# A one-core encoder layer on Trainium2: turning the gated features on VectorE and by transfers inside SBUF instead of on TensorE, with fewer seven-product pairs

## The chip, the core and the metric

The kernel runs on one core of one Trainium2 chip. A core has TensorE (PE in the profile; its weight loads are listed as PEld), VectorE (DVE), ScalarE (ACT), GpSimd (POOL) and SyncE (SP, which here only issues DMAs), sixteen DMA engines, a software-managed SBUF of 128 partitions, and PSUM, in which matmuls accumulate. The metric is the device time of one execution in microseconds (us). Several runs were taken of the kernel before, and one further execution was profiled; the trace has the start and the end of every instruction of that one.

## What is computed

One layer of an encoder for 256 positions (S) with 2048 features (D), all in float32:

```
u      = rms_norm(h) @ w_in                      # 2048 x 5120
mixed  = concat(rms_norm(attention), rms_norm(recurrence)) @ w_out
h      = h + rms_norm(mixed)
fn     = rms_norm(h)
ff     = (silu(fn @ w_gate) * (fn @ w_up)) @ w_down      # 2048 -> 5632 -> 2048
h      = h + rms_norm(ff)
h      = h + rms_norm(sigmoid(rms_norm(h) @ w_ple_gate) * (p @ w_ple_proj))
```

The change touches the line with `w_gate`, `w_up` and `w_down` (the FFN). Its middle features, silu(gate) * up, come out with positions on the partitions, and `w_down` needs them with features on the partitions: they have to be transposed.

## The kernel before

**Products.** Each float32 operand is split in a rounded part `hi` and the rest `lo`, and a product is three matmuls: hi by hi, hi by lo, lo by hi. A weight tile is 256 rows by 512 columns (128 partitions x 1024 elements, 512 KB). SP loads it into a raw slot (L439), ACT makes `wh` (L464), DVE makes `wl` (L489), and PE uses both (L528 to L530). Raw slots ("wr") and split slots ("w") are few and are lent and given back through the kernel; a load waits for a raw slot, and a cast for a split slot.

**Groups.** The FFN works in groups of two weight chunks of 512 columns (gate and up, or two chunks of w_down). A group takes its 256-row steps, called units or pairs, one after another. A "p" unit is plain: two weight tiles, 24 matmuls of 512 columns. An "s" unit forms the same 2 x 2 blocks of products by seven products in place of eight (`seven`, L546): 21 matmuls, but two further weight tiles, which DVE makes as sums and differences of the first two (`sum_stream`, L509 and L513, four subtractions of 512 elements), and which have to be cast and split as well. On the side of the activations such a unit needs four sums of position blocks (`act_sums`). `KINDS` says which of the eight units of a gate/up group are "s", and `DOWN` gives order and kind of the units of a down group.

**The FFN's order.** Eleven gate/up groups (`Gated`) in three parts: groups 0 to 3, 4 to 7 and 8 to 10. After each part come two down groups (`Down`) for the features just made; after the last part one down group and two plain chunks.

**The end of a gate/up group.** `Seven.early` and `Gated.late` add up what the seven products left in PSUM (L1553 to L1565, L1589), put silu on the gate half (L1616) and multiply with the up half (L1596), all with positions on the partitions. Then `transposed` (L307) has PE turn the result in blocks of 128 x 128 into a PSUM bank, four at a time (L315), twice a group, and `split` (L292) makes hi and lo of each bank (ACT L295, DVE L297). For the "s" units of the down groups, `mid_sums` adds hi and lo again (L1390) and forms the four sums (L1466) and their hi and lo.

**What sets the order.** The program's instruction order on each engine is made by a planner (`Plan`) when the kernel is built. It has a clock for each engine with estimated costs; a step is a generator that yields (engine, cost, slot to take or give), and of all steps that could go the one that starts earliest is taken, with `late` added to its start (a negative value brings it forward). On the chip each engine then works through its instructions strictly in that order and waits by semaphores where the real times differ from the planned ones. This holds for SP too: all loads and stores of the layer go through its one queue in planned order.

Of the kernel before, what the change touches and what calls it, by code (L numbers as in the profile page):

```python
# [43 lines left out]
for _n, _w in (  # L44
# [23 lines left out]
LATE_SUMS = 0.0  # L68
FIRST = "ppppspsp"
KINDS = "ppspspsp"  # L70
HALF = max(2 * KINDS.count("s") * 4 * P, 2 * 1024)
# [156 lines left out]

def dma(kb, take=None):
    return ("dma", kb / 340.0, None, take, None)  # L230
# [3 lines left out]
def layer(ctx: ExitStack, tc: tile.TileContext, a: dict, out: bass.AP):  # L234
# [6 lines left out]
        wr=R_BUFS, w=W_BUFS, ts=0, acc=ACC_BUFS, sm=SM_BUFS, ev=1, mid=2, bt=2, uv=1  # L241
# [36 lines left out]
    ones = const.tile([P, P], F32, name="ones")  # L278
    nc.gpsimd.memset(ones, 1.0)
# [50 lines left out]
    def done(event):  # L330
        event.t = plan.now
# [11 lines left out]
    class Act:  # L343
# [10 lines left out]
        def blocks(self, hi, lo, base, n, first=0):  # L354
            for i in range(n):
                self.at[base + i] = (hi[:, first + i, :], lo[:, first + i, :])
# [18 lines left out]
    class Group:  # L375


        def __init__(self, w, n0, lhs, ks, kinds, post, after=None):
            self.after = after
            self.lhs, self.post, self.banks, self.i0 = lhs, post, {}, len(tiles)  # L380
            self.early = Event()
            self.units = list(zip(ks, kinds))
            self.early = Event()
            for (k, _), kind in self.units:
                i = len(tiles)
                tiles.extend((w[c], k, n0[c]) for c in range(2))
                by_dma.update({"d": (i, i + 1), "e": (i + 1,), "c": (i,)}.get(kind, ()))
                if kind == "s":
# [82 lines left out]
    def add_raw(i):  # L471
        yield added(512)
        nc.gpsimd.dma_start(los[i], raws[i], accum_op=ALU.add)
        landed = Event()
        landed.t = plan.now + LANDED
        yield landed
        done(ev_lo[i, 2])
        used(i)
# [40 lines left out]
    def products(i, kx, lhs, accs, ts, start, stop, at=0.0):  # L519
        for j in range(2):  # L520
            here = ev_lo[i, j + 1] if (i, j + 1) in ev_lo else ev_lo[i, 2]
            plan.main(6 * MM * len(ts) / NT, here, lhs.ev[kx + j], at=at)
            wh, wl = his[i], los[i]
            hi, lo = lhs.at[kx + j]
            for t in ts:
                sl = slice(t * P, (t + 1) * P)
                st, sp = start and j == 0, stop and j == 1
                nc.tensor.matmul(accs[t], hi[:, sl], wh[:, j, :], start=st, stop=False)  # L528
                nc.tensor.matmul(accs[t], hi[:, sl], wl[:, j, :], start=False, stop=False)  # L529
                nc.tensor.matmul(accs[t], lo[:, sl], wh[:, j, :], start=False, stop=sp)  # L530
            at_pe[0] = max(at_pe[0], i)
            if j:
                free_w(i)
            plan.run()
# [11 lines left out]
    def seven(i, kx, g, start, stop):  # L546

        for name, v, j, which in FORMS:
            n = i + v
            if isinstance(which, tuple):  # L550
                kk, t = which
                (hi, lo), ev = g.lhs.at[kx + kk], g.lhs.ev[kx + kk]
                hi, lo = hi[:, t * P : (t + 1) * P], lo[:, t * P : (t + 1) * P]
# [14 lines left out]
    def run_group(g, flip):  # L568
# [5 lines left out]
        strassens = [n for n, (_, kind) in enumerate(g.units) if kind == "s"]  # L574
        for n, ((_, kx), kind) in enumerate(g.units):
            if kind == "s":
                seven(i, kx, g, n == strassens[0], n == strassens[-1])
                i += 4
                if n == strassens[-1]:
                    plan.add(g.post.early(g), plan.clk["pe"] + plan.SEM)  # L580
                    plan.run()
                continue
# [7 lines left out]
        plan.add(g.post.late(g), plan.clk["pe"] + plan.SEM)  # L590
# [139 lines left out]
    def open_p1():  # L730
        t1["hs"], t1["rec_hi"] = big(0, "hs", F32), big(1, "rec_hi")
        p1 = p1_ctx.enter_context(tc.tile_pool(name="p1", bufs=1))
        t1["pool"] = p1
        xp = p1.tile([P, HB, S + 4], F32, name="xp")
# [23 lines left out]
        nc.gpsimd.memset(ssr, 0.0)  # L758
# [3 lines left out]
    ssr = const.tile([P, S], F32, name="ssr")  # L762
    ssa = const.tile([P, S], F32, name="ssa")
# [151 lines left out]
    def group_rstd(ss, name):  # L915
# [3 lines left out]
        nc.tensor.matmul(pb[:, 0, :], ones, ss, start=True, stop=True)  # L919
        rb = const.tile([P, S], F32, name=f"rb_{name}")  # L920
# [15 lines left out]
    def gate_pair(b0, b, e, ev):  # L936
# [9 lines left out]
        yield from add_squares(ssr, sq, False)  # L946
        done(ev)

    def yg_post(hf):
        def post(ch):  # L950
# [13 lines left out]
            rb = yield from group_rstd(ssr, "rec")  # L964
# [132 lines left out]
    def attend(g):  # L1097
        ph, pl, vh, vl, sq, attnT = (t1[n] for n in ("ph", "pl", "vh", "vl", "sqa", "attnT"))
        yield ev_v[g]
        for b in range(0, HB, 2):  # L1100
# [23 lines left out]
            yield from add_squares(ssa, sq, h == 0)  # L1124
# [3 lines left out]
        ra = yield from group_rstd(ssa, "attn")  # L1128
# [39 lines left out]
    def open_p2():  # L1168
# [12 lines left out]
        for n in range(W_MORE):  # L1181
# [3 lines left out]
            plan.free["w"].append(plan.clk["pe"])  # L1185
        plan.add(load_p2(), plan.clk["pe"])
# [191 lines left out]
    def mid_sums(mid, ks):  # L1378
        rs = t2["pool"]
        a_ = rs.tile([P, 2, 2, 4, P], F32R, tag="ple0", name="sums_a")  # L1380
        b_ = rs.tile([P, 2, 4, P], F32R, tag="pT", name="sums_b")
        at_ = [(a_[:, n, 0, :, :], a_[:, n, 1, :, :]) for n in range(2)]
        at_.append((b_[:, 0, :, :], b_[:, 1, :, :]))
        for k, (hi, lo) in zip(ks, at_):
            mid.sums[k] = hi, lo
            yield mid.ev[k]
            yield mid.ev[k + 1]
            yield dve(2 * S, take="uv")
            v = at.tile([P, 2, NT, P], F32, tag="at0_hi", name="v")
            nc.vector.tensor_tensor(  # L1390
                out=v.rearrange("p k t m -> p k (t m)"), in0=f32(mid.pair_of(k, 0)),
                in1=f32(mid.pair_of(k, 1)), op=ALU.add,
            )
            yield from act_sums(mid, k, v)

# [18 lines left out]
    def transpose_h(b, hi, lo, nxt, gname):  # L1414
# [20 lines left out]
        yield from act_sums(nxt, b, v)  # L1435
# [20 lines left out]
    def act_sums(x, b, v):  # L1456

        s = at.tile([P, 4, P], F32, tag="at0_lo", name="s")
        for n, i0, i1, op in (
            (0, v[:, 0, 1, :], v[:, 1, 1, :], ALU.add),  # L1460
            (1, s[:, 0, :], v[:, 0, 0, :], ALU.subtract),
            (2, v[:, 0, 0, :], v[:, 0, 1, :], ALU.subtract),
            (3, v[:, 1, 0, :], s[:, 1, :], ALU.subtract),
        ):
            yield dve(P)
            nc.vector.tensor_tensor(out=s[:, n, :], in0=i0, in1=i1, op=op)  # L1466
# [63 lines left out]
    class Mid(Act):  # L1530
        def __init__(self, name):
            super().__init__()
            self.name, self.halves = name, {}
# [8 lines left out]
        def pair_of(self, k, which):  # L1542
            i, j = divmod(k, 8)
            return self.halves[i][which][:, j : j + 2, :]
# [31 lines left out]
    class Gated(Seven):  # L1576
# [5 lines left out]
        def late(self, g):  # L1582
# [3 lines left out]
            gated = [Event() for _ in range(NT)]  # L1586
            for t, c, n, x in self.parts():
                yield dve(N)
                nc.vector.tensor_tensor(out=x, in0=bk[n], in1=x, op=ALU.add)  # L1589
                g.give(n)  # L1590
                if not c:
                    plan.add(self.silu(t, gated[t]), plan.now)
            for t in range(NT):
                yield gated[t]
# [4 lines left out]
                )  # L1599
            plan.free["uv"].append(plan.now)  # L1600
            for b in range(0, 4, 2):
                tr = yield from transposed(e, b, g.ring["c11"])
                if b == 2:
                    plan.free["mid"].append(plan.now)
                kk = self.kk0 + b
                i, j = divmod(kk, 8)
                hi, lo = self.mid.tiles(i)
# [5 lines left out]
        def silu(self, t, ev):  # L1613
# [34 lines left out]
    hF.ev_sums = {k: Event() for k, kind in zip(ORDER, KINDS) if kind == "s"}  # L1648

    parts = ((0, 4), (4, 8), (8, 11))  # L1650
    for part, (f0, f1) in enumerate(parts):
        mid = Mid(f"mid{part}")
        for f in range(f0, f1):
            Group(("w_ffn_gate", "w_ffn_up"), (f * N, f * N), hF,
                  [(k, k) for k in ORDER], KINDS if f else FIRST, Gated(mid, (f - f0) * 4))
        last_lent[0] = len(tiles)
        last = part == len(parts) - 1
        units = [[(u[0], int(u[1:])) for u in us.split()] for us in DOWN[f1 - f0]]
        summed = []
        for us in units[:1] if last else units:  # L1660
            summed += [k for kind, k in us if kind == "s" and k not in summed]
        mid.ev_sums = {k: Event() for k in summed}
        for n in range(1 if last else 2):
# [3 lines left out]
                  after=(lambda mid=mid, ks=summed: plan.add(  # L1667
                      mid_sums(mid, ks), plan.clk["pe"], LATE_SUMS)) if n == 0 else None)
# [189 lines left out]
```

## Time and profile before

| what | value |
|---|---|
| runs before (three) | 1175.58, 1175.52, 1174.06 us, median 1175.52 us |
| the profiled execution, its own time | 1173.45 us |
| its span, first to last instruction | 1171.7 us |
| mean granted TensorE clock | 0.997 |
| ACT busy | 701.9 us, 60% of the span |
| DMA queue of SP | 237.79 MB, 60.9% of sixteen engines' span |
| FFN groups | about 377 us to 1055 us of the span |

The profile lists instructions by source line and by tile names, written as output<-inputs. "idle before" is the time that an engine stood still just before such instructions, with what ended the wait. Matmuls overlap in the trace (each is shown as 0.39 us long, though a new one starts every 0.23 us), so for PE it is the distance of the starts that counts.

### The profile page before, as it was taken

The numbers are of one execution on the slowest core, as the hardware profiler recorded it, in microseconds if no ns is written. First come the engines' busy times: TensorE is split into PE (matmuls) and PEld (weight loads), VectorE is DVE, ScalarE is ACT, GpSimd is POOL, SyncE is SP. The second block draws the span as 40 slices with busy tenths as digits, with TensorE's granted clock in tenths as the row PEclk, the third lists the DMA queues.
The fourth block names the chain that finished last, engine by engine and source line by source line (L and its number), as shares of the span: only waits on it lengthen the run. The fifth ranks groups of instructions, "written<-read, shape, count | busy, mean of one in ns | idle before, by whom it ended". The sixth has DMA issues, their size and how long they took to land.

```text
span 1171.7 us, 14652 instructions
## 1 busy us (share of the span) xinstructions
PE 1150.5 (98%) x5259; PEld 951.6 (81%) x5259; DVE 961.3 (82%) x1267; ACT 701.9 (60%) x952; POOL 1.6 (0%) x13
## 2 busy tenths in 40 slices
PE   7999999999999999999999999999999999999996
PEld 5788888888888888888888888888888888887885
DVE  5677868778549898898989899889999989888663
ACT  6787777766548655563665556554536446466752
POOL 0000000000000000000000000000000000000000
PEclk9999999999999999999999999999999999999998
DMA  8855555545864865664775475575567456775751
GB/s 307 288 173 180 176 187 197 164 158 168 313 229 141 302 191 180 224 214 146 226 256 192 159 245 182 173 238 160 191 207 242 153 180 229 261 246 190 241 171 72
DMA packets 70344, 238.80 MB, mean 204 GB/s; under 512 B 7552, under 2 KB 13824, under 8 KB 68864
## 3 DMA queue, kind: packets, MB, share of 16 engines
q1 hardware_dynamic: 70128, 237.79, 60.9%
q8 instruction: 41, 0.67, 0.2%
q14 instruction: 31, 0.25, 0.1%
q10 hardware_dynamic: 144, 0.08, 0.0%
HBM read 232.60 MB, written 5.24 MB: 203 GB/s over the span
## 4 chain that ended last, share of the span: by engine, by line
PE 82%; DVE 6%; DMA 6%; ACT 3%; issue 1%; SPq 1%; DVEq 0%; ACTq 0%
PE c L528 12%; PE c L530 12%; PE c L529 12%; PE acc L530 9%; PE acc L528 9%; PE acc L529 9%; PE p L538 3%; PE p L539 3%; PE p L537 3%; DVE wl L489 3%; PE c L537 2%; PE c L538 2%; PE c L539 2%; PE tr L315 2%; DMA wr<-in_w_ffn_down 1%; DMA xs<-in_xT 1%
## 5 line engine op out<-in xcount | busy, mean ns | idle before, releaser
L489 DVE TENSOR_TENSOR wl<-wr,wh 128x1024 fp32r<-128x1024 f32 (+1 forms) x311 | 358.4, 1167 | 76.0 <-ACT wh L464 75.1
L464 ACT CAST wh<-wr 128x1024 fp32r<-128x1024 f32 (+1 forms) x311 | 307.8, 1008 | 138.8 <-PE acc L530 46.7
L528 PE MATMUL c<-wh,hT_mix_hi 128*128 128x512 f32 x400 | 157.4, 394 | 0.0
L530 PE MATMUL c<-wh,hT_mix_lo 128*128 128x512 f32 x400 | 155.9, 390 | 0.0
L529 PE MATMUL c<-wl,hT_mix_hi 128*128 128x512 f32 x400 | 155.8, 389 | 0.0
L464 ACT CAST wh<-lent_t 128x1024 fp32r<-128x1024 f32 x75 | 78.7, 1052 | 113.0 <-DVE lent_t L513 105.7
L528 PE MATMUL acc<-wh,hT_hi 128*128 128x512 f32 x320 | 127.9, 400 | 6.6 <-ACT wh L464 6.6
L529 PE MATMUL acc<-wl,hT_hi 128*128 128x512 f32 x320 | 125.6, 392 | 1.8 <-DVE wl L489 1.8
L530 PE MATMUL acc<-wh,hT_lo 128*128 128x512 f32 x320 | 125.5, 392 | 0.0
L489 DVE TENSOR_TENSOR wl<-lent_t,wh 128x1024 fp32r<-128x1024 f32 x75 | 89.6, 1218 | 1.3 <-ACT wh L464 1.1
L530 PEld LDWEIGHTS c<-wh,hT_mix_lo 128*128 128x128 f32 x400 | 75.1, 188 | 16.0 <-DVE hT_mix_lo L303 0.2
L529 PEld LDWEIGHTS c<-wl,hT_mix_hi 128*128 128x128 f32 x400 | 75.2, 188 | 15.0
L528 PEld LDWEIGHTS c<-wh,hT_mix_hi 128*128 128x128 f32 x400 | 75.1, 188 | 15.0
L489 DVE TENSOR_TENSOR wl<-lent_r,wh 128x1024 fp32r<-128x1024 f32 (+1 forms) x70 | 76.3, 1102 | 4.7 <-ACT wh L464 4.5
L464 ACT CAST wh<-lent_r 128x1024 fp32r<-128x1024 f32 (+1 forms) x70 | 65.1, 957 | 23.9 <-PE c L530 15.2
L528 PEld LDWEIGHTS acc<-wh,hT_hi 128*128 128x128 f32 x320 | 60.6, 189 | 18.1 <-ACT wh L464 6.6
L529 PEld LDWEIGHTS acc<-wl,hT_hi 128*128 128x128 f32 x320 | 60.4, 189 | 14.9 <-DVE wl L489 3.4
L530 PEld LDWEIGHTS acc<-wh,hT_lo 128*128 128x128 f32 x320 | 60.3, 189 | 12.7
L530 PE MATMUL acc<-wh,hT_ffn_lo 128*128 128x512 f32 x112 | 43.7, 390 | 0.9 <-DVE hT_ffn_lo L303 0.9
L528 PE MATMUL acc<-wh,hT_ffn_hi 128*128 128x512 f32 x112 | 44.0, 393 | 0.0
L529 PE MATMUL acc<-wl,hT_ffn_hi 128*128 128x512 f32 x112 | 43.6, 389 | 0.0
L1616 ACT ACTIVATE mid<-mid,rstd_f 128x512 f32<-128x512 f32 x22 | 14.7, 716 | 28.8 <-DVE mid L1589 28.8
(439 smaller groups left out, 2334.8 us busy)
## 6 DMA issues: line engine op xcount, KB each, us to landing
wr<-in_w_in SPq DMA_DIRECT2D x79, 512.0 KB, 4.4
wr<-in_w_ffn_down SPq DMA_DIRECT2D x68, 512.0 KB, 4.3
wr<-in_w_ffn_gate SPq DMA_DIRECT2D x60, 512.0 KB, 4.2
wr<-in_w_ffn_up SPq DMA_DIRECT2D x60, 512.0 KB, 4.7
wr<-in_w_out SPq DMA_DIRECT2D x32, 512.0 KB, 4.7
wr<-in_w_ple_gate SPq DMA_DIRECT2D x32, 512.0 KB, 4.3
lent_r<-in_w_ffn_gate SPq DMA_DIRECT2D x28, 512.0 KB, 4.2
lent_r<-in_w_ffn_up SPq DMA_DIRECT2D x28, 512.0 KB, 4.5
```

The source lines that it names most:

```text
L315: nc.tensor.transpose(tr[:, b, t * P : (t + 1) * P], src, ident)
L464: nc.scalar.copy(his[i][:, j, :], raws[i][:, j, :])
L489: nc.vector.tensor_tensor(out=los[i][:, j, :], in0=raws[i][:, j, :], in1=f32(his[i][:, j, :]), op=ALU.subtract,)
L528: nc.tensor.matmul(accs[t], hi[:, sl], wh[:, j, :], start=st, stop=False)
L529: nc.tensor.matmul(accs[t], hi[:, sl], wl[:, j, :], start=False, stop=False)
L530: nc.tensor.matmul(accs[t], lo[:, sl], wh[:, j, :], start=False, stop=sp)
L537: nc.tensor.matmul(o, lh, wh, start=start, stop=False)
L538: nc.tensor.matmul(o, lh, wl, start=False, stop=False)
L539: nc.tensor.matmul(o, ll, wh, start=False, stop=stop)
L1616: nc.scalar.activation(self.e[:, t, :], self.e[:, t, :], AF.Silu, scale=rstd_f[:, t : t + 1])
```

## The change

Five things are changed together.

1. In `Gated.late`, the gated features `e` (128 positions x 2 position blocks x 512 features) are turned by DVE in blocks of 32 x 32 in place (`nc.vector.transpose`), and sixteen DMAs on SP's queue move the blocks from partition group to partition group inside SBUF into `raw` (new function `turn`, 32 KB each: 32 partitions x 2 runs of 512 bytes). One cast and one subtraction of 1024 elements then make hi and lo. The PE transposes of the gated features are gone. The features come out in another order within their block of 512, and the rows of `w_down` are reordered to match before the launch.
2. `mid_sums` is gone. The sums for "s" units of the down groups are made in `Gated.late` from `raw`, without adding hi and lo again.
3. Fewer "s" units: gate/up groups 1, 2, 5 and 8 have two and not three (group 0 had two before), and the second down group of the first two parts has two and not three. The order of the down units is changed as well.
4. One raw slot of 4 KB per partition more from the start of the output projection on (`R_MORE`); some tiles of the first half are moved to a pool that is closed earlier.
5. Planner figures: `TURN` 4.0 us for the sixteen DMAs, `TURN_LATE` -4.0, `LANDED` 6.0 in place of 2.5; the four adds at the end of a group are steps of their own (`sum_up`).

```diff
-LANDED = 2.5
+LANDED = 6.0
+TURN = 4.0
+TURN_LATE = -4.0
 DOWN = {
-    4: ("p2 p6 p10 p8 s0 p12 s4 p14", "p2 p6 s0 p10 s4 p12 s8 p14"),
-    3: ("p2 p6 p10 s0 p4 p8", ""),
+    4: ("p2 p6 s0 p8 p10 s4 p12 p14", "p2 p6 s0 p10 s4 p12 p8 p14"),
+    3: ("p2 p4 s0 p6 p8 p10", ""),
 }
 FIRST = "ppppspsp"
-KINDS = "ppspspsp"
+KINDS = tuple("ppspspsp" if f == "3" else "ppppspsp" for f in "32233233233")
+R_MORE = 1
...
+def turn():
+    return ("dma", TURN, None, None, None)
...
+        for which, n, tag in (("ts", T_MORE, "ts"), ("wr", R_MORE, "wr")):
+            for m in range(n):
+                slots[which].append(lambda tag=tag, m=m: rs.tile(
+                    [P, 2, N], F32, tag=f"{tag}_{m}", name=tag, bufs=1))
+                plan.free[which].append(plan.clk["pe"])
...
-    def mid_sums(mid, ks):
-        rs = t2["pool"]
...
-            nc.vector.tensor_tensor(
-                out=v.rearrange("p k t m -> p k (t m)"), in0=f32(mid.pair_of(k, 0)),
-                in1=f32(mid.pair_of(k, 1)), op=ALU.add,
-            )
-            yield from act_sums(mid, k, v)
...
+        def open(self):
+            rs = t2["pool"]
+            both = rs.tile([P, 2, 4 * S], F32, tag="ple0", name="turned")
+            self.raw = both[:, 0, :].rearrange("p (t a n) -> p t a n", a=4, t=NT)
...
             for t in range(NT):
-                yield gated[t]
+                for ev in gated[t]:
+                    yield ev
                 yield dve(N)
                 nc.vector.scalar_tensor_tensor(
                     out=e[:, t, :], in0=u[t], scalar=rstd_f[:, t : t + 1], in1=e[:, t, :],
                     op0=ALU.mult, op1=ALU.mult,
                 )
+            yield dve(2 * N)
+            nc.vector.transpose(e, e)
             plan.free["uv"].append(plan.now)
+            n = self.kk0 // 4
+            if not n:
+                self.mid.open()
+            raw = self.mid.raw
+            there = Event()
+            plan.add(self.turn(e, raw, there), plan.now, TURN_LATE)
+            yield there
+            plan.free["mid"].append(plan.now)
+            i, j = divmod(self.kk0, 8)
+            hi, lo = (x[:, j : j + 4, :].rearrange("p b (c i) -> p c b i", i=32)
+                      for x in self.mid.tiles(i))
+            raw = raw.rearrange("p t a (b i) -> p (t a) b i", b=4)
+            yield from split(hi, lo, raw, 2 * N)
             for b in range(0, 4, 2):
-                tr = yield from transposed(e, b, g.ring["c11"])
...
-                yield from split(
-                    hi[:, j : j + 2, :], lo[:, j : j + 2, :], tr, 2 * S, give=g.ring["c11"]
-                )
-                self.mid.pair(kk)
+                self.mid.pair(self.kk0 + b)
+            for k in self.mid.ev_sums:
+                if self.kk0 <= k < self.kk0 + 4:
+                    b = k - self.kk0
+                    yield dve(1, take="uv")
+                    yield from act_sums(
+                        self.mid, k, lambda j, t: raw[:, 4 * t : 4 * t + 4, b + j, :], "p (a i) -> p a i"
+                    )
+
+        def turn(self, e, raw, there):
+            yield turn()
+            for c in range(4):
+                for a_ in range(4):
+                    nc.sync.dma_start(
+                        raw[c * 32 : (c + 1) * 32, :, a_, :],
+                        e[a_ * 32 : (a_ + 1) * 32, :, c * P : (c + 1) * P],
+                    )
+            done(there)
...
+        if n == "w_ffn_down":
+            w = w.reshape(k // N, 4, 4, 32, m).transpose(0, 2, 1, 3, 4).reshape(k, m)
```

More of the change, by code (lines that the diff above doesn't have):

```diff
@@ L355, in blocks @@
             for i in range(n):
-                self.at[base + i] = (hi[:, first + i, :], lo[:, first + i, :])
+                self.at[base + i] = tuple(
+                    [x[:, first + i, t * P : (t + 1) * P] for t in range(NT)] for x in (hi, lo)
+                )
     class Chunk:
@@ L469, in hi_stream, with add_to @@
                 plan.add(add_raw(i), plan.now)
-    def add_raw(i):
-        yield added(512)
-        nc.gpsimd.dma_start(los[i], raws[i], accum_op=ALU.add)
+    def add_to(out, src, kb):
+        yield added(kb)
+        plan.clk["dma"] = max(plan.clk["dma"], plan.now - ADDED) + SHARED * kb / 512
+        nc.gpsimd.dma_start(out, src, accum_op=ALU.add)
         landed = Event()
@@ L733, in open_p1 @@
         t1["pool"] = p1
+        t1["ones"] = p1.tile([P, P], F32, name="ones")
+        nc.gpsimd.memset(t1["ones"], 1.0)
         xp = p1.tile([P, HB, S + 4], F32, name="xp")
@@ L918, in group_rstd @@
         pb = bank(f"pb_{name}")
-        nc.tensor.matmul(pb[:, 0, :], ones, ss, start=True, stop=True)
-        rb = const.tile([P, S], F32, name=f"rb_{name}")
+        nc.tensor.matmul(pb[:, 0, :], t1["ones"], ss, start=True, stop=True)
+        rb = t1["pool"].tile([P, S], F32, name=f"rb_{name}")
         yield act(S, SQRT, give="sm")
@@ L1585, in late @@
             e, u = self.e, self.u
-            gated = [Event() for _ in range(NT)]
+            gated = [[Event() for _ in range(2)] for _ in range(NT)]
             for t, c, n, x in self.parts():
[L1588 to L1592, printed above, removed]
+                plan.add(self.sum_up(g, n, t, c, x, gated[t][c]), plan.now)
             for t in range(NT):
-                yield gated[t]
+                for ev in gated[t]:
+                    yield ev
                 yield dve(N)
@@ L1646, in after_ffn @@
         return next_norm(ffn, hP, rstd_p, ev_rp, ("ple", "g_ple_post"))
-    hF.ev_sums = {k: Event() for k, kind in zip(ORDER, KINDS) if kind == "s"}
+    hF.ev_sums = {k: Event() for k, kind in zip(ORDER, ALL) if kind == "s"}
     parts = ((0, 4), (4, 8), (8, 11))
     for part, (f0, f1) in enumerate(parts):
-        mid = Mid(f"mid{part}")
+        mid = Mid(f"mid{part}", 4 * (f1 - f0))
+        units = [[(u[0], int(u[1:])) for u in us.split()] for us in DOWN[f1 - f0]]
+        last = part == len(parts) - 1
+        summed = []
+        for us in units[:1] if last else units:
+            summed += [k for kind, k in us if kind in "st" and k not in summed]
+        mid.ev_sums = {k: Event() for k in summed}
         for f in range(f0, f1):
             Group(("w_ffn_gate", "w_ffn_up"), (f * N, f * N), hF,
-                  [(k, k) for k in ORDER], KINDS if f else FIRST, Gated(mid, (f - f0) * 4))
+                  [(k, k) for k in ORDER], KINDS[f % len(KINDS)] if f else FIRST, Gated(mid, (f - f0) * 4))
         last_lent[0] = len(tiles)
[L1657 to L1662, printed above, removed]
         for n in range(1 if last else 2):
```

105 lines of the change are left out of this document (52 added, 53 removed).

## The prediction

> **What bounds the kernel now.** I read the page first, then the FFN in stretches, then the lists by line, the chain in order of time, SP's waits, and last the timeline of single engines where a transposed block is made. The page's shares, and one row of its groups:
>
> ```profile
> PE 1150.5 (98%) x5259; PEld 951.6 (81%) x5259; DVE 961.3 (82%) x1267; ACT 701.9 (60%) x952; POOL 1.6 (0%) x13
> ...
> L528 PE MATMUL c<-wh,hT_mix_hi 128*128 128x512 f32 x400 | 157.4, 394 | 0.0
> ```
>
> PE is busy 98% of the span, and the gate/up matmuls (c<-wh,hT_mix) never had idle time before them: the 0.0 at the row's end. Busy time of overlapping matmuls could hide small waits, so I look at the pace. The columns are PE, PEld, DVE, ACT and POOL busy, the clock, the DMA share and GB/s:
>
> ```profile
> 412.00:545.00 133.00, 133.00 (x604) 110.17 (x603) 121.20 (x150) 76.05 (x88) 0.00 (x0) 1.00 0.59 195
> 545.00:618.00 73.00, 73.00 (x324) 60.42 (x323) 69.32 (x87) 37.86 (x42) 0.00 (x0) 1.00 0.68 223
> ...
> 871.00:997.00 126.00, 126.00 (x565) 104.38 (x564) 115.64 (x138) 68.27 (x77) 0.00 (x0) 1.00 0.59 198
> 997.00:1055.00 58.00, 58.00 (x262) 48.02 (x261) 49.30 (x63) 32.18 (x43) 0.00 (x0) 1.00 0.73 252
> 800.00:870.00 70.00, 70.00 (x310) 57.96 (x309) 65.64 (x82) 37.20 (x41) 0.00 (x0) 1.00 0.64 210
> ```
>
> From 800 to 870 there are only 512-column matmuls: 310 in 70 us is one per 0.226 us (0.227 if the two cut by the edges are not counted). In every stretch PE is full, so the FFN lasts as long as its matmuls and transposes take. DVE is next: 121.20 of 133 us is 91%, 69.32 of 73 is 95%. So a matmul or transpose fewer shortens the kernel by its own time, as long as DVE, ACT and SP stay ahead.
>
> **What is removed on PE.** The chain in order of time shows the gated blocks' transposes, first and last of 22 such sets of four (two a group, eleven groups):
>
> ```profile
> 412.72 0.44 PE tr L315 x4
> ...
> 1007.47 0.45 PE tr L315 x4
> ```
>
> 22 x 0.44 = 9.7 us leave PE's path.
>
> **What is added on PE.** A unit made plain has 24 matmuls and not 21. Six units change: four in gate/up groups 1, 2, 5 and 8, one in each second down group of the first two parts. 6 x 3 x 0.227 = 4.1 us. Net on PE: -9.7 + 4.1 = -5.6 us, if nothing waits.
>
> **DVE and ACT.** The rows for the FFN from 377 to 1055 us, by line (busy, mean ns, idle before):
>
> ```profile
> L489 DVE TENSOR_TENSOR wl<-lent_t,wh 128x1024 fp32r<-128x1024 f32 x75 | 89.6, 1218 | 1.3 <-ACT wh L464 1.1
> L509 DVE TENSOR_TENSOR lent_t<-wr 128x512 f32<-128x512 f32 x28 | 19.1, 683 | 0.5 <-DMA wr<-in_w_ffn_up 0.5
> L297 DVE TENSOR_TENSOR mid1l<-tr,mid1h 128x512 fp32r<-128x512 f32 x8 | 5.5, 691 | 5.1 <-ACT mid1h L295 5.0
> L1466 DVE TENSOR_TENSOR s<-v 128x128 f32<-128x128 f32 x16 | 4.6, 286 | 0.4 <-ACT v L1431 0.2
> L1390 DVE TENSOR_TENSOR v<-mid0h,mid0l 128x512 f32<-128x512 f32 x3 | 2.0, 683 | 0.0
> L464 ACT CAST wh<-lent_t 128x1024 fp32r<-128x1024 f32 x75 | 78.7, 1052 | 113.0 <-DVE lent_t L513 105.7
> L295 ACT CAST mid1h<-tr 128x512 fp32r<-128x512 f32 x8 | 4.7, 586 | 12.0 <-PE tr L315 11.6
> ```
>
> A seven-product unit costs, beside a plain one, one and a half weight tiles more to split (two sums, less half of the second tile) and four subtractions: on DVE 1.5 x 1.22 + 4 x 0.68 = 4.5 us, on ACT 1.5 x 1.05 = 1.6 us. Six fewer give DVE back 27 us and ACT 9.5 us. The seven adds of L1390 go (seven sums in all: three, three and one), 7 x 0.68 = 4.8 us, and two of the seven sets of sums, 2 x (4 x 0.29 + 0.68) = 3.7 us. The two subtractions of 0.69 per group become one of 1024 elements, like the 1.22 of L489: 11 x (1.22 - 1.38) = -1.8 us. ACT's two casts of 0.59 become one of about 1.05, in place of 1.17.
>
> The trace has no 32 x 32 turning. It reads and writes 128x1024 elements; the half-size row (0.68) is the lower bound, twice the 1.22 row the upper (2.4), and I take 1.2, for a VectorE pass over as many elements. 11 x 1.2 = 13 us. DVE's sum is 13 - 27 - 4.8 - 3.7 - 1.8 = -24 us over the FFN, at the upper bound -11. But it isn't even: a group that keeps three "s" units gets 1.0 us more DVE work (at most 2.3) on 0.9 us less PE time, a group that loses one gets 3.5 us less. DVE isn't the path before; with less work in total its change costs nothing.
>
> **The sixteen DMAs.** They are the part that can take the gain back. Nearest rows: the gate loads, four DMAs of 128 KB issued in a row (first and last), and DMAs with KB and median us to landing:
>
> ```profile
> 144.07 0.43 SPq L808 DMA_DIRECT2D av<-in_w_rg_a  x1
> ...
> 145.57 0.47 SPq L808 DMA_DIRECT2D av<-in_w_rg_i  x1
> wr<-in_w_ffn_gate SPq DMA_DIRECT2D x60, 512.0 KB, 4.2
> av<-in_w_rg_a SPq DMA_DIRECT2D x8, 128.0 KB, 4.1
> kept_ple<-ple SPq DMA_DIRECT2D x1, 1024.0 KB, 3.8
> out<-h SPq DMA_DIRECT2D x2, 128.0 KB, 1.9
> ```
>
> One issue takes SP 0.43 to 0.47 us, so sixteen hold its queue 6.9 to 7.5 us; I take 7.2. The last lands 1.9 to 4.1 us after its issue; I take 3.8, the row that reads SBUF. From turning to landing that is 11 us (8.8 to 11.6), where the planner reckons TURN 4.0 plus 2.0. So in ACT's queue the cast of the turned block stands up to 5 us too early, with the casts of the next weight tiles behind it; and on SP the weight loads wait behind the sixteen issues, and behind the wait for DVE's turning, which TURN_LATE puts ahead of loads that could go up to 4 us sooner. GpSimd's queue carries none of this.
>
> What hides it is the time between a load and its use. One group's end, counting loads and casts in their order: SP's queue, DVE's last multiply, the cast of the load of 752.03, PE's first use of it:
>
> ```profile
> 739.45 0.33 SPq L439 DMA_DIRECT2D wr<-in_w_ffn_up  x1
> 752.03 0.33 SPq L439 DMA_DIRECT2D wr<-in_w_ffn_gate  x1
> 756.84 0.33 SPq L439 DMA_DIRECT2D lent_r<-in_w_ffn_gate  x1
> 746.90 0.74 DVE L1596 SCALAR_TENSOR_TENSOR mid<-u_lo,rstd_f,mid 128x512 f32<-128x512 f32 x1
> 760.22 2.00 ACT L464 CAST wh<-wr 128x1024 fp32r<-128x1024 f32 x2
> 770.75 0.39 PE L528 MATMUL c<-wh,hT_mix_hi 128*128 128x512 f32 x1
> ```
>
> SP issues nothing from 739.8 to 752.03: it waits for a raw slot. The multiply ends at 747.64, the turning would end at 748.8, and the sixteen issues fill 748.8 to 756.0, mostly inside that hole. The load of 752.03 would go at 756.0, 4 us late; it lands 4.2 us later, at 760.2, when its cast ran anyway. To be late for PE at 770.75 it would have to be over 9 us late (4.2 landing, 1.05 cast, 1.22 subtraction, and some 3 for what stands before them, leave 9 of 18.7). The extra raw slot, one tile or 2.7 us of PE work (12 x 0.227), moves loads forward by as much. I cost the DMAs at 0 in such groups.
>
> The cover is thin elsewhere. DVE's subtraction against the PE use of its tile, early in the FFN and in the last down group:
>
> ```profile
> 418.09 2.35 DVE L489 TENSOR_TENSOR wl<-lent_t,wh 128x1024 fp32r<-128x1024 f32 x2
> 419.61 0.39 PE L537 MATMUL p<-wh,sums_f 128*128 128x512 f32 x1
> 1016.24 3.62 DVE L489 TENSOR_TENSOR wl<-wr,wh 128x1024 fp32r<-128x1024 f32 x3
> 1019.34 0.39 PE L528 MATMUL c<-wh,mid2h 128*128 128x512 f32 x1
> ```
>
> The first of the two ends at about 419.3, 0.3 us before use; the first of the three at about 1017.4, 1.9 us before. A delay of 2 to 3 us there is paid by PE. Early on, groups 1 and 2 give DVE 3.5 us each, more than such a delay; at the end no unit is saved. I charge 0.6 us in all.
>
> **Is the turned block itself in time?** The tightest place is the last gate/up group, whose features PE needs from unit p8 on:
>
> ```profile
> 997.31 0.39 PE L528 MATMUL c<-wh,mid2h 128*128 128x512 f32 x1
> 999.57 0.74 DVE L1596 SCALAR_TENSOR_TENSOR mid<-u_lo,rstd_f,mid 128x512 f32<-128x512 f32 x1
> 997.00 0.43 SPq L1402 DMA_DIRECT2D h<-kept  x1
> 1007.86 6.94 SPq L439 DMA_DIRECT2D wr<-in_w_ffn_down  x4
> ```
>
> The down group starts at 997.31. The features are ready at 1000.31, turned at 1001.5, issued by 1008.7 (SP was empty from 997.43 to 1007.86), landed at 1012.5, cast and subtracted by 1014.8. In the new order p2 p4 s0 p6 p8, three plain units and one of seven come first: 93 x 0.227 = 21.1 us, until 1018.4. That leaves 3.6 us. In the other parts six units come first, 138 x 0.227 = 31.3 us.
>
> **The sum.** Span 1171.7 - 9.7 + 4.1 + 0.6 = 1166.7 us; the profiled execution took 1173.45, 1.75 more than its span, so 1168.5. The median of the runs, 1175.52, is 2.07 above that execution, and I forecast against the median: 1170.5 us.
>
> **The rivals.** About 0.2% (2.35 us) is what a measurement of this kernel can tell from no change.
>
> *The thin places pay.* The cast of the turned block waits up to 5 us more than planned in ACT's queue; where the lead is 0.3 to 2 us and not 9, PE stands. For it: the two thin rows, and that three-"s" groups run DVE fuller. Against it: the holes on SP, and DVE's 24 us. Of eleven groups some four (1, 2, 3 and 10) have such leads; 1.4 us each in place of 0.6 in all gives +5.0 us: 1175.5, no change.
>
> *SP's queue becomes the bound.* The sixteen issues, each with 64 short rows, take SP longer than a gate load, the planned order puts loads behind them, and every group waits. It decides from about 13 us of holding on (the 4 us that loads are late at 7.2, plus 5 more that use up the 9): 0.8 us an issue. At 0.9 us, 14.4 in all, PE loses some 2 us more in each of ten groups on top of the thin places' 5: 1175.5 + 20 = 1196, slower; near the threshold just above 1178. For it: no row shows a DMA from SBUF to SBUF of 32 partitions. Against it: 0.43 to 0.47 us is what every strided issue took.
>
> *The transfers go one after another.* If each is paid whole, sixteen cost 16 x 1.9 = 30.4 us from the row of 128 KB. Then the last part's block is there at 1001.5 + 30.4 + 2.3 = 1034.2, 15.8 us after 1018.4, and in the other parts (4.2 after the group's end, 30.4, 2.3: 36.9 against 31.3) 5.6 us late twice: +27, so 1197, slower. Against it, from this case: 128 KB takes 4.1 and 512 KB 4.2 to land, and the four gate loads are issued 0.5 us apart while each needs 4, so transfers overlap. [...]
>
> **How the numbers follow.** Forecast, cover holds and 0 to 2.7 us are lost: 0.59, own range 1169.5 to 1172.6. Better than that, since the transposes also held ACT and DVE in line: 0.04. Thin places pay, 1173.2 to 1177.8: 0.20. SP bound: 0.13. One after another: 0.04. So faster 0.63, same 0.20, slower 0.17. The range takes in the first three cases and leaves out the slower ones: 1168 to 1177.9.
>
> **What would show it.** PE instructions: 5259 - 88 + 18 = 5189. Right: the FFN stretches stay full for PE at 0.227 us a matmul, and a group lasts 0.9 us less, or 0.2 less where it lost an "s" unit. Wrong on SP: issues of `raw` at over 0.8 us each, or L439 landing late with PE idle behind ACT's casts. Wrong on the landing: idle time on ACT's cast of the turned block of over 5 us. Wrong on DVE: the turning at over 2.4 us. What would prove the forecast wrong as a whole is idle time of PE in the FFN of over 3 us.

## The result, and the profile after

| | before | after |
|---|---|---|
| median of the runs, us | 1175.03 (1174.06 to 1175.58, four runs) | 1205.36 (1205.03 to 1207.67, four runs) |
| ratio after / before | | 1.0263 (95%: 1.0245 to 1.0281) |
| span of the profiled execution, us | 1171.7 | 1203.0 |
| mean granted TensorE clock | 0.997 | 0.988 |

The changed kernel is 2.6% slower, 30.3 us, where 1170.5 was forecast and the range ended at 1177.9. All that is lost is lost in the FFN: from the first gate/up matmul behind the transposes of `h` to the last matmul with `w_down` takes 694.6 us before and 727.7 after.

The page of the changed kernel: busy time, the shares of the chain that ended last, one group of gate/up matmuls, and the row of the sixteen DMAs (KB each, median us to landing):

```profile
PE 1157.9 (96%) x5189; PEld 952.6 (79%) x5189; DVE 941.7 (78%) x1214; ACT 689.4 (57%) x927; POOL 1.6 (0%) x13
...
PE 62%; DVE 17%; SPq 8%; DMA 5%; issue 4%; ACT 4%; DVEq 0%; ACTq 0%
...
L544 PE MATMUL c<-wl,hT_mix_hi 128*128 128x512 f32 x436 | 171.5, 393 | 9.4 <-DVE wl L505 9.4
...
turned<-mid SPq DMA_DIRECT2D x176, 32.0 KB, 1.9
```

PE issues 5189 instructions, exactly 88 transposes less and 18 matmuls more, and yet is busy 7 us longer. The group of gate/up matmuls, which never stood before, now stands 9.4 us for DVE's low halves of weight tiles. The stretch table of the FFN, before and after (columns as in the prediction):

```profile
368.00:1063.00 695.00, 694.93 (x3109) 575.04 (x3108) 629.59 (x778) 386.69 (x460) 0.00 (x0) 1.00 0.63 208
```

```profile
368.00:1096.00 728.00, 703.01 (x3039) 575.82 (x3038) 611.67 (x728) 375.01 (x435) 0.00 (x0) 0.98 0.62 207
```

DVE has 18 us less to do and ACT 12, as forecast in direction, but PE is no longer full: 728.0 less 703.0 is 25 us of standing, and 70 instructions fewer take 8 us more. That is two losses, one of time without a matmul and one of slow matmuls. Counted from the distances of the starts of the 512-column matmuls from 350 to 1100 us, pauses of over 0.6 us beyond that distance sum to 25.9 us in eleven places (before: 1.1 in one), and what is slower than one per 0.227 us outside pauses to 14.5 us (before: 4.3). So -5.6 for the work on PE, +24.8 for pauses and +10.2 for slow matmuls make +29.4, where the FFN grew by 33.1 and the span by 31.3; 2 to 4 us are not located.

Who stands first is in the list of waits (us in all, times, longest). All its rows about the turned block, and PE's largest that come of them:

```profile
ACT mid0h L305 <- DMA turned<-mid: 24.8, 4, 7.2
ACT mid1h L305 <- DMA turned<-mid: 23.0, 4, 6.0
DVE mid0l L307 <- ACT mid0h L305: 22.4, 4, 6.4
DVE mid1l L307 <- ACT mid1h L305: 22.1, 4, 6.0
...
ACT mid2h L305 <- DMA turned<-mid: 17.7, 3, 6.1
DVE mid2l L307 <- ACT mid2h L305: 17.2, 3, 6.1
...
PE c L544 <- DVE wl L505: 11.1, 5, 4.9
```

Eleven groups, eleven stands: ACT 65.5 us, 6.0 a group; DVE behind it 61.7 us, 5.6 a group. Why 6 is in the instructions of the line of the sixteen DMAs (shortest/median/longest issue in ns, first and last start) and of the turning:

```profile
L1639 SPq DMA_DIRECT2D turned<-mid x176: 587/595/1346, 413.2 to 1044.9; - x176
```

```profile
L1610 DVE STREAM_TRANSPOSE mid<-mid x11: 1233/1236/1246, 411.9 to 1034.0; 128x1024 f32<-128x1024 f32 x11
```

The turning takes 1.24 us (1.2 forecast). An issue takes 0.595 us, not 0.45, and one starts every 0.64: sixteen hold SP for 10.2 us (10.9 at most). Each lands 1.9 us after its issue began, so the last lands 1.3 us after the hold ends and 11.5 us after the turning (11.5 to 12.2 in the eleven groups), where the planner reckons 4.0 + 2.0. The wait of the queues is about the difference, 5.5 to 6.2.

One group's end shows how that reaches PE. The timelines of SP, ACT, DVE and PE (start, duration, instruction; in brackets the idle time before it and what ended it):

```profile
983.26 0.33 SPq L451 DMA_DIRECT2D wr<-in_w_ffn_gate  x1
989.83 10.20 SPq L1639 DMA_DIRECT2D turned<-mid  x16
1000.14 0.52 SPq L451 DMA_DIRECT2D wr<-in_w_ffn_up  x1
```

```profile
993.79 2.00 ACT L476 CAST wh<-lent_r 128x1024 fp32r<-128x1024 f32 x2
1001.42 1.04 ACT L305 CAST mid2h<-turned 128x1024 fp32r<-128x1024 f32 x1 [5.64 <-DMA turned<-mid]
```

```profile
988.57 1.23 DVE L1610 STREAM_TRANSPOSE mid<-mid 128x1024 f32<-128x1024 f32 x1
...
996.19 0.68 DVE L525 TENSOR_TENSOR lent_t<-wr,lent_t 128x512 f32<-128x512 f32 x1
1002.50 1.22 DVE L307 TENSOR_TENSOR mid2l<-turned,mid2h 128x1024 fp32r<-128x1024 f32 x1 [5.62 <-ACT mid2h L305]
1003.64 1.22 DVE L505 TENSOR_TENSOR wl<-lent_r,wh 128x1024 fp32r<-128x1024 f32 x1
```

```profile
999.62 0.39 PE L543 MATMUL c<-wh,hT_mix_hi 128*128 128x512 f32 x1
1004.91 0.80 PE L544 MATMUL c<-wl,hT_mix_hi 128*128 128x512 f32 x1 [4.90 <-DVE wl L505]
1005.50 0.63 PE L545 MATMUL c<-wh,hT_mix_lo 128*128 128x512 f32 x1
```

The subtraction `wl` that PE waits for has had all its inputs since 995.8, when ACT's cast ended. It is done at 1004.86, because the subtraction of the turned block stands ahead of it in DVE's queue, waiting for ACT's cast, which waits for the last of the sixteen DMAs. Nobody needs the turned block yet. Then comes the second loss; the stretches before, in and behind this pause:

```profile
995.00:999.60 4.60, 4.60 (x22) 3.81 (x21) 1.88 (x3) 0.78 (x1) 0.00 (x0) 1.00 0.21 54
999.60:1004.90 5.30, 0.41 (x2) 0.00 (x0) 2.40 (x3) 3.46 (x4) 0.00 (x0) 0.88 0.69 218
1004.90:1010.00 5.10, 5.09 (x12) 4.03 (x13) 5.10 (x7) 3.89 (x4) 0.00 (x0) 0.50 0.87 301
```

The granted clock is 0.50 behind the pause: 12 matmuls in 5.1 us, against 22 in 4.6 ahead of it.

### The profile page after: what moved, and what is told of

Same layout as the page of the kernel before. It is cut to its first block, busy times and chain, and to the rows that moved or that the text cites. A ratio compares the mean times of both kernels' runs of the same rounds, so it can differ in the third digit from the quotient of the medians.

```text
span 1203.0 us, 14688 instructions
## 1 busy us (share of the span) xinstructions
PE 1157.9 (96%) x5189; PEld 952.6 (79%) x5189; DVE 941.7 (78%) x1214; ACT 689.4 (57%) x927; POOL 1.6 (0%) x13
## 4 chain that ended last, share of the span: by engine, by line
PE 62%; DVE 17%; SPq 8%; DMA 5%; issue 4%; ACT 4%; DVEq 0%; ACTq 0%
PE acc L545 10%; PE acc L544 10%; PE acc L543 10%; SPq L1639 7%; PE c L544 7%; PE c L545 7%; PE c L543 7%; DVE wl L505 6%; ACT wh L476 2%; DMA turned<-mid 1%; PE p L553 1%; PE p L554 1%; PE p L552 1%; DVE lent_t L529 1%; DVE lent_w L505 1%
## 5 line engine op out<-in xcount | busy, mean ns | idle before, releaser
L505 DVE TENSOR_TENSOR wl<-wr,wh 128x1024 fp32r<-128x1024 f32 (+1 forms) x319 | 367.8, 1170 | 78.3 <-ACT wh L476 77.7
L476 ACT CAST wh<-wr 128x1024 fp32r<-128x1024 f32 (+1 forms) x319 | 315.6, 1010 | 139.6 <-PE acc L545 60.0
L544 PE MATMUL c<-wl,hT_mix_hi 128*128 128x512 f32 x436 | 171.5, 393 | 9.4 <-DVE wl L505 9.4
L543 PE MATMUL c<-wh,hT_mix_hi 128*128 128x512 f32 x436 | 171.4, 393 | 1.7 <-DVE mid L1568 1.7
L545 PE MATMUL c<-wh,hT_mix_lo 128*128 128x512 f32 x436 | 171.2, 393 | 0.0
L476 ACT CAST wh<-lent_t 128x1024 fp32r<-128x1024 f32 x65 | 68.1, 1052 | 120.2 <-DVE lent_t L529 93.0
L544 PEld LDWEIGHTS c<-wl,hT_mix_hi 128*128 128x128 f32 x436 | 82.6, 189 | 27.6 <-DVE wl L505 10.6
L545 PEld LDWEIGHTS c<-wh,hT_mix_lo 128*128 128x128 f32 x436 | 82.7, 190 | 17.5 <-DVE hT_mix_lo L313 0.2
L505 DVE TENSOR_TENSOR wl<-lent_t,wh 128x1024 fp32r<-128x1024 f32 x65 | 78.4, 1218 | 12.5 <-ACT wh L476 12.1
L505 DVE TENSOR_TENSOR wl<-lent_r,wh 128x1024 fp32r<-128x1024 f32 (+1 forms) x61 | 68.3, 1130 | 10.0 <-ACT wh L476 9.9
L543 PE MATMUL c<-wh,mid1h 128*128 128x512 f32 x88 | 34.9, 397 | 3.1 <-ACT wh L476 3.1
```

Source lines behind the costliest of these rows:

```text
L476: nc.scalar.copy(his[i][:, j, :], raws[i][:, j, :])
L505: nc.vector.tensor_tensor(out=los[i][:, j, :], in0=raws[i][:, j, :], in1=f32(his[i][:, j, :]), op=ALU.subtract,)
L543: nc.tensor.matmul(accs[t], hi[t], wh[:, j, :], start=st, stop=False)
L544: nc.tensor.matmul(accs[t], hi[t], wl[:, j, :], start=False, stop=False)
L545: nc.tensor.matmul(accs[t], lo[t], wh[:, j, :], start=False, stop=sp)
```

## The experiments

My theory after the result: one wrong price, `TURN`, puts the cast and the subtraction of the turned block 6 us too early into two queues that work in order, and all else follows. The rivals: SP's hold makes the weight loads late; the transfers themselves disturb; or the other parts of the change (fewer "s" units, the raw slot, the new order) cost. Every comparison is with the kernel before on the same chip (medians 1175.71 to 1176.13); two changed kernels that are compared can have run on different chips.

**The price alone.** The diff against the changed kernel:

```diff
-TURN = 4.0
+TURN = 10.2
```

> The changed kernel with the planner's price TURN raised from 4.0 to 10.2 us, the time that the sixteen issues held SP in its trace (0.64 us each); nothing else. Theory (wrong price: ACT and DVE meet the cast of the turned block 6 us too early in their queues and stand): those waits go from about 6 us a group to under 1.5, PE's pauses of 26 us and the halved clock behind them go, and the time is 1175 - 5.6 = 1168 to 1173 us. Rival (SP's hold of 10 us itself makes the weight loads late, whatever the planned order): PE pauses stay and the time is 1185 us or more.

Measured: 1165.80 us, ratio 0.9907 (0.9890 to 0.9925), span 1164.0, clock 0.998. The list of waits and the FFN's stretch:

```profile
ACT mid2h L305 <- DMA turned<-mid: 4.9, 2, 4.0
...
ACT mid0h L305 <- DMA turned<-mid: 4.7, 3, 1.8
...
ACT mid1h L305 <- DMA turned<-mid: 2.9, 2, 1.9
```

```profile
369.00:1057.00 688.00, 688.00 (x3038) 569.44 (x3037) 613.29 (x727) 378.01 (x435) 0.00 (x0) 1.00 0.65 220
```

The same instructions in another order are 40 us faster, and faster than before. The time is 2 us better than I had expected. ACT's stands fall from 65.5 to 12.5 us and PE is full again, busy 688.00 of 688.00 us, though SP still issues the same 176 DMAs. So neither the hold of SP nor the transfers need cost PE anything.

**Which half of the price: the loads behind the issues?** Here the price stays 4.0, but the planner is told when the block lands, so that the cast comes in time and only the loads are planned against an SP that is believed free.

```diff
-            done(there)
+            there.t = plan.now + 6.2
```

> The changed kernel with only the consumers planned 6.2 us later (the event that releases the cast of the turned block), while TURN stays 4.0 and with it the planned order of SP's queue. Theory (the early place of the cast in ACT's and DVE's queues is what costs): 1168 to 1176 us, waits of ACT for the turned block under 1.5 us a group. Rival (the loads planned with a free SP are late because it is held 6 us longer): casts of weight tiles wait for their DMAs instead, and the time stays at 1190 us or more.

Measured: 1196.34 us, ratio 1.0170 (1.0154 to 1.0185). My theory's number for this run was wrong, and the rival was right here. The list of waits:

```profile
DVE lent_t L525 <- DMA wr<-in_w_ffn_up: 29.9, 9, 6.2
ACT wh L476 <- DMA wr<-in_w_ffn_down: 27.3, 12, 7.9
...
DVE lent_t L525 <- DMA wr<-in_w_ffn_down: 13.8, 3, 6.9
DVE lent_t L525 <- DMA lent_r<-in_w_ffn_up: 12.9, 5, 6.2
```

ACT stands only 9.4 us for the turned block now; DVE and ACT stand for weight loads instead, up to 7.9 us. Loads that the plan believes on their way wait behind 10.2 us of issues, and the instructions that use them are placed too early in the same two queues. PE's longest pause, 5.4 us until 1041.6, is for the turned block after all, but its cast stands behind two that wait 5.8 and 2.1 us for weight loads.

**Which half: the early cast?** The price is right, so SP's queue is planned right, but the planner believes the landing 6.2 us too early.

```diff
-TURN = 4.0
+TURN = 10.2
...
-            done(there)
+            there.t = plan.now - 6.2
```

> TURN 10.2, so that SP's queue is planned with its true hold, but the cast of the turned block is planned 6.2 us earlier, where the changed kernel has it. It is the other half of the run with only the consumers later (1196 us). Theory of two halves: the early cast alone costs ACT and DVE about 6 us a group, and the time is 1185 to 1205 us. Rival (only the placement of the loads matters): 1166 to 1172 us.

Measured: 1206.06 us, ratio 1.0249 (1.0233 to 1.0265), as slow as the change itself. The list of waits:

```profile
ACT mid0h L305 <- DMA turned<-mid: 25.3, 4, 7.2
ACT mid1h L305 <- DMA turned<-mid: 22.4, 4, 5.9
...
ACT mid2h L305 <- DMA turned<-mid: 17.7, 3, 6.4
```

The same three rows as in the change, within 0.6 us. So the early cast alone makes the whole loss; late loads alone make three quarters of it (1196.34 and 1205.36 against 1165.80 with both right, +30.5 of +39.6); together they make no more than the first. Both fill the same hole, a stand of some 6 us in ACT's and DVE's queues once a group.

**Half the error.** The price in the middle:

```diff
-TURN = 4.0
+TURN = 7.1
```

> The changed kernel with TURN 7.1, half way between the planner's 4.0 and the measured 10.2. If the loss follows the error of the price by a threshold (it is hidden until the lead is used up): 1168 to 1176 us, nearer to 1166 than to 1205. If it is proportional to the error: 1183 to 1188 us.

Measured: 1173.76 us, ratio 0.9979 (0.9967 to 0.9991). The list of waits:

```profile
ACT mid0h L305 <- DMA turned<-mid: 14.3, 4, 5.2
...
ACT mid2h L305 <- DMA turned<-mid: 12.9, 3, 6.0
...
ACT mid1h L305 <- DMA turned<-mid: 11.1, 4, 2.9
```

Half the error leaves 38.3 us of ACT's standing, 3.5 a group, yet costs 8 us of the 40. The loss isn't in proportion. The stretch of the first experiment shows DVE busy 613.29 of 688 us; for each of the eleven groups, with its share of the down groups, 6.8 us are free. It can stand 3.5 with little harm, but not 5.6 on top of its uneven load. That DVE's free time sets the threshold fits both numbers and was not tried by itself. The clock has a part in it: PE's pauses here are 1.1 us of idle time at the longest, and the mean granted clock is 0.997, as before, where the change has 0.988.

**Another queue for the DMAs.** The sixteen go through GpSimd's queue, in unchanged order and with the price unchanged:

```diff
-                    nc.sync.dma_start(
+                    nc.gpsimd.dma_start(
```

> The changed kernel with the sixteen transfers issued by GpSimd instead of SP; planned order unchanged. It takes the hold off SP's queue and leaves the early place of the cast. If SP's hold is the cause: 1168 to 1176 us. If the early place of the cast is: as slow as the landing is late; with landing 12 us after the turning, as on SP, 1200 us or more, and slower still if GpSimd issues more slowly than 0.64 us each.

Measured: 1223.88 us, ratio 1.0406 (1.0390 to 1.0421). SP's queue is free, and the kernel is slower still. From the lists of DMA issues and of waits:

```profile
turned<-mid POOLq DMA_DIRECT2D x176, 32.0 KB, 4.3
```

```profile
ACT mid0h L305 <- DMA turned<-mid: 33.8, 4, 9.8
...
ACT mid1h L305 <- DMA turned<-mid: 27.2, 4, 7.8
...
ACT mid2h L305 <- DMA turned<-mid: 20.4, 3, 8.7
```

Landing takes 4.3 us there, not 1.9, and ACT stands 81.4 us in place of 65.5. The time follows the stands of ACT, not the load of SP. The same with the order right: the hold planned at 2.0, the landing put 9.4 us after it.

```diff
-TURN = 4.0
+TURN = 2.0
...
-                    nc.sync.dma_start(
+                    nc.gpsimd.dma_start(
...
-            done(there)
+            there.t = plan.now + 9.4
```

> Transfers issued by GpSimd, as in the run before, but the planner is told what that run showed: the cast of the turned block is planned 13.4 us after the turning (TURN 2.0, the planner's 2.0, and 9.4), so that neither SP's loads nor the cast are misplaced. Theory (two misplacements, both from the price, and nothing in the transfers themselves): 1163 to 1169 us, like the run with TURN 10.2. Rival (512-byte transfers in flight beside the weight loads slow those, wherever they are issued): 1180 us or more.

Measured: 1166.83 us, ratio 0.9913 (0.9891 to 0.9936), 57 us less than with the old order. Queue and landing time (4.5 us in the median here) hardly matter once the order knows them: the ratio is 0.9913 against 0.9907 with SP's queue. Nor do the transfers as such hold PE up: in the first experiment it was busy 688.00 of 688.00 us with all 176 of them.

**The other parts without the turning.** The kernel before, with the new `KINDS`, `DOWN`, raw slot and pools, and the PE transposes kept:

```diff
...
-KINDS = "ppspspsp"
+KINDS = tuple("ppspspsp" if f == "3" else "ppppspsp" for f in "32233233233")
...
+R_MORE = 1
...
```

> The kernel before with only the fewer seven-product units, the new order of the down units and the extra raw slot; the gated features still turned by PE, sums as before. Theory: PE gets 18 matmuls more, 4.1 us, and nothing else moves: 1178 to 1180 us. Rival (the order of the down units or the unit kinds cost more than their matmuls): over 1183 us.

Measured: 1176.36 us in ten runs, ratio 1.0003 (0.9993 to 1.0012): +0.4 where 18 matmuls more let me expect +4.1. The rival, that these parts make the loss, falls. The profiled spans differ by 3.8 (1175.5 against 1171.7), and the FFN of the two profiled executions by 3.7, close to the 4.1. But the profiled execution of before lies below its own median there and this one above its own; whether the medians or the spans tell the true cost stays open.

**Fewer "s" units, with the right price.** All groups keep three:

```diff
-TURN = 4.0
+TURN = 10.2
...
-KINDS = tuple("ppspspsp" if f == "3" else "ppppspsp" for f in "32233233233")
+KINDS = tuple("ppspspsp" if f == "3" else "ppppspsp" for f in "33333333333")
```

> TURN 10.2 and three seven-product units again in gate/up groups 1, 2, 5 and 8: 12 matmuls fewer on PE (2.7 us), 18 us more work for DVE in these four groups. If DVE keeps ahead: 1162 to 1164 us. If DVE has become the bound in groups of three: over 1168 us.

Measured: 1165.85 us, ratio 0.9907 (0.9887 to 0.9927), the same median as with two, and between my two forecasts. Its profiled span of 1162.2 is 1.8 shorter, but the four spans with two run from 1162.3 to 1164.0, and these from 1162.2 to 1166.2. Its FFN stretch:

```profile
369.00:1056.00 687.00, 685.78 (x3021) 566.31 (x3021) 627.79 (x748) 380.96 (x442) 0.00 (x0) 1.00 0.66 220
```

DVE has 14.5 us more to do, PE 12 matmuls less (5177 on its page), and PE is as good as full. Giving up "s" units bought nothing that a run could tell.

**The raw slot, with the right price.**

```diff
-TURN = 4.0
+TURN = 10.2
...
-R_MORE = 1
+R_MORE = 0
```

> TURN 10.2 without the additional raw slot. If the slot is what lets the loads run ahead of SP's hold of 10 us: PE pauses in each group, 1175 us or more. If the right planned order is enough: 1165 to 1170 us.

Measured: 1189.94 us, ratio 1.0111 (1.0087 to 1.0136). The slot is worth 24 us. PE stands 17 us in pauses, in some groups and not in each, and the FFN lasts 708.1 us. The likely reason is that no load starts while SP is held for 10.2 us, and that without the slot too few are under way: behind the sixteen issues that end at 515.5 us five loads leave one after another. It was not followed from there to each pause of PE.

**What makes an issue long.** Each of the sixteen is cut in two, with one run of 512 bytes for each partition and not two; the price is 13.0. There is one run of it:

```diff
-TURN = 4.0
+TURN = 13.0
...
-                    nc.sync.dma_start(
-                        raw[c * 32 : (c + 1) * 32, :, a_, :],
-                        e[a_ * 32 : (a_ + 1) * 32, :, c * P : (c + 1) * P],
-                    )
+                    for t in range(NT):
+                        nc.sync.dma_start(
+                            raw[c * 32 : (c + 1) * 32, t, a_, :],
+                            e[a_ * 32 : (a_ + 1) * 32, t, c * P : (c + 1) * P],
+                        )
```

> What an issue costs SP: each of the sixteen transfers is made two of 16 KB, 32 rows of one run of 512 bytes (TURN 13.0 to match). If the second run per row makes the issue 0.6 us, these take 0.33 to 0.40 each, about 12 us a group; if the form with 32 partitions does, they stay at 0.55 to 0.6, about 19 us a group, and the time goes over 1185 us.

Measured: 1249.5 us. The instructions of the line, and one group on SP's timeline:

```profile
L1640 SPq DMA_DIRECT2D turned<-mid x352: 512/589/1674, 413.3 to 1089.1; - x176
```

```profile
512.07 20.14 SPq L1640 DMA_DIRECT2D turned<-mid  x32
```

Half the bytes and one dimension less take 0.59 us an issue and 0.63 from start to start: the hold doubles to 20.1 us. So in this form the price is paid for each DMA: 0.589 us with half the bytes and one run, against 0.595. What in this form costs more than a weight load's 0.33 us stays open. (The loss here holds both a longer hold and a price again too low.)

## Why the prediction was wrong

- **Work on PE**, -9.7 + 4.1 = -5.6: right in the count (5189) and, where the order is right, a little small. With the price at 10.2 the FFN takes 687.8 us against 694.6, -6.8. The parts taken singly: the turning in place of the transposes is worth 10.6 (1176.36 less 1165.80; the new sums and `sum_up` are in it, which no run tried alone), the plain units cost 0.4 or 3.8, by the medians or the spans.
- **The turning**, 1.2 us: right, 1.24. DVE's total fell by 18 us in the FFN, within the 11 to 24 of the two ends.
- **The sixteen issues**: the term was mis-sized, 0.45 us from the gate loads (which take 0.38 to 0.47), measured 0.595 and 0.64 apart. The hold is 10.2 us and not 7.2. Landing was bounded by 1.9 and 4.1, and I took 3.8 as "the row that reads SBUF"; but the row `out<-h` reads SBUF too, with the 1.9 that came out. From turning to landing 11.5 us passed, where 11 was forecast: the two errors nearly cancel, and the delay that mattered was sized about right.
- **"In ACT's queue the cast of the turned block stands up to 5 us too early"**: right, ACT stands 6.0 us a group for it. I saw the place, and lost it in the next step.
- **The step that failed** is the one behind "What hides it is the time between a load and its use" and "I cost the DMAs at 0 in such groups". It measured the cover of one load, 18.7 us from issue to use, and asked whether that load would come over 9 us late. But what the early cast uses up isn't the cover of a load. It is the time of ACT and, behind it, of DVE: both work in order, so for 5.6 us a group DVE makes no weight tile at all, in the group shown with all inputs there. The prediction had DVE at 91 to 95% of stretches in which PE was full, and "DVE isn't the path before; with less work in total its change costs nothing" counted its work and not its standing. Against the 18 us of work that DVE was spared stand 61.7 us of waiting. Nor does the cover of a load hold by itself: where the cast was planned in time and only the loads came late, ACT and DVE stood up to 7.9 us for them (second experiment).
- **"I charge 0.6 us in all"** and the rival of the thin places, 5.0: the mechanism of that rival is the one that came about, but it was put at some four groups and 1.4 us each. All eleven groups stood, and PE lost 24.8 us more in pauses than before.
- **SP's queue as the bound**: it was to decide from 13 us of holding on (its own terms, 7.2 and 5, give 12.2). With the order planned for it, 10.2 us cost nothing (first experiment); with an order that believes SP free, the same hold costs 30 us (second, against the first). So there is no such threshold in the hold as such: what decides is the hold against the price in the plan, and whether the slots carry PE over it (without the extra one 24 us are lost). Its 1196 and the second experiment's 1196.34 agree by chance.
- **One after another**: refuted, as forecast. The sixteen start 0.64 us apart and each lands after 1.9. The last landed 11.5 us after the turning, where 16 x 1.9 is 30.4.
- **Not foreseen at all**: the price of slow matmuls behind a pause, 10.2 us of the 30.
- Two signs that the prediction named came out: idle time on ACT's cast over 5 us, and PE idle in the FFN over 3 us. But the first was to mean a landing sized wrong, and it came with a landing sized about right.

Priced rightly, the change gives 1165.8 us, 4.7 us better than the forecast for it. Some of that is the time around the transposes that the prediction gave a chance of 0.04: matmuls slower than their pace outside pauses summed to 4.3 us before, and to about 2 with the price at 10.2.

## What to carry to other kernels

Where the order of engines is written out ahead by a planner, the price of a new step is part of the change: compare it with the whole time from issue to landing, and read what stands behind the waiting instruction in its queue, not only whether its result is needed in time. An engine that is 91% busy has little time to stand, however much work it is spared; an instruction placed 6 us too early in its queue, once a group, cost 40 us here, and moved to its true place next to nothing. The small DMAs of this change are paid in issues on the queue that starts them (0.595 us each, 10.2 us for sixteen), so measure one issue of the very form first.

## What the runs showed of the hardware

**The clock behind a pause.** In or shortly behind some pauses of PE the granted clock falls to half, for 3.41 us or twice that: in the changed kernel 3.41 us from 518.9, 781.7 and 826.1, and 6.83 us from 734.0 and 1003.6, with starts 0.427 us apart in place of 0.227. From one beginning to the next it is 63, 14, 13 and 52 times 3.413 us. The shortest pause that has such a piece with it in this kernel is 2.8 us of idle time:

```profile
734.77 0.80 PE L553 MATMUL p<-lent_w,hT_mix_hi 128*128 128x512 f32 x1 [2.80 <-DVE lent_w L505]
```

This one and the pause of 4.90 us (until 1004.91) have 6.83 us at half clock with them, those of 3.53 us (until 518.97), 3.75 us (until 780.38) and 3.10 us (until 823.96, with 0.95 more until 825.41) have 3.41 us, and 1.74 us (until 494.52) has none. In the run with only the early cast 1.90 us of idle time (until 520.59) was enough: starts shortly behind it (521.23, 521.65) are 0.42 us apart. So the length of a pause alone does not decide how long the clock stays down, and a stand of some 3 us on PE can cost twice: behind the 2.80 us, 14 matmuls took 6.09 us from start to start, where 14 x 0.227 is 3.18.

**The issue of a small transfer.** 32 KB from SBUF to SBUF take SP 0.595 us to issue, more than 512 KB from the layer's weights (0.33), and GpSimd's queue lands the same transfer in 4.3 us in the median where SP's takes 1.9. One start is 0.595 of the 1.9 us from issue to landing, and sixteen starts hold the queue for 10.2 us.
